# Delta rule's triangular inverse: diagonal blocks of 16 eliminated row by row on VectorE for all heads and segments at once

## The chip, the cores and the metric

The kernel runs on one core of a Trainium2 chip, in one launch. The metric is the device time of that core in microseconds (us); lower is better. Five engines work side by side: TensorE (PE) multiplies matrices, VectorE (DVE) and ScalarE (ACT) work elementwise and read out what TensorE left, GpSimd (POOL) does little here, and SyncE (SP) issues the DMAs. Engines run their own instructions in order and wait for one another by semaphores.

## The reference

Two blocks of two layers each run over 256 tokens of width 1024 in float32. In the first block 16 meta tokens stand ahead, so a layer has 272. Its mixer joins two branches: sparse attention, whose keys an index of eight small heads selects, and the gated delta rule with four heads of 128 and a per-token decay. The change is in the delta rule of the first block's two layers. Cut to what matters, per chunk and head:

```python
kk = einsum('bhncd,bhnsd->bhncs', kc, kc)
m = where(strict, bc[..., None] * kk * decay, 0.0)    # strictly lower
lhs = m + eye(CHUNK)
sol = triangular_solve(lhs, rhs, lower=True, unit_diagonal=True)
...                                  # then a scan over the chunks carries the state S
```

The result does not depend on the length of a chunk. The kernel uses its own: three segments of 16, 128 and 128 tokens.

## The kernel before

**Dense products.** Nearly all of the time goes to products of weights with activations, tokens as columns. A weight comes by DMA in pieces of 1 MB (`raw`, two buffers). ScalarE copies a 128x1024 stretch as `whi` (L261), VectorE subtracts that from `raw` to get `wlo` (L262), four buffers each, and TensorE takes three products per 128x128 tile: `whi` with the high part of the activations, `whi` with the low part, `wlo` with the high part (L287, L288, L289). So one split on VectorE feeds eight products on L289.

**Side chains.** Everything else of a mixer is written as generators. The function `dense` calls `tick()` twice per block of 128 output columns, and each tick takes every running chain to its next `yield`. So a chain's instructions stand in each engine's queue between dense products, in the order of the ticks. The projections are issued in the order of this line (L1077), where `k`, `q`, `v` are the delta rule's projections through a short convolution, `i` the index's queries, `b`, `K` and `kv` the attention's, `S` starts the attention's chain, `D` the delta rule's, and `g` and `z` are gates:

```python
for name in (begin + " k1 g1 q0 g2 q1 D i0 i1 S kv K v0 b0 v1 b1 g3 z0 z1 g4 g5 g6 g7").split():
```

After them the branch products follow, first the attention's, then (once all chains have ended) the delta rule's.

**The delta rule.** The chain `delta` waits for the sums of squares of q and k and makes their scales. Then it takes `part1(0)` and `scan(0)` for the 16 tokens, `part1(1)` and `part1(2)` in turn (a step of the one, a step of the other, then a yield for both), `scan(1)` and `scan(2)`. In `part1(s)` a step is four small float32 products, one for each head, into one PSUM bank `psn` (of which there are two), and an operation on VectorE or ScalarE that reads it:

1. the decays DT from the cumulated gates, four products, four VectorE operations, an exponential;
2. kk, and four VectorE operations that make MT, the transposed strictly lower matrix;
3. the inverse of (I + M), transposed as XT. It starts from the pairs (masks `lev1` and the identity), transposes to Xm (L752), and then takes a radix round (L765 with mask `rad`, then three steps of L771 with subtractions L775, L776) that joins four blocks into one: on blocks of 2 and on blocks of 8 for the large segments, on blocks of 2 alone for the 16-token one. Each round ends with a transposition. A half level joins blocks of 32 (of 8 in the small segment) by two product steps (L797 the first), and in the large segments a transposition and two more product steps join the two halves of 64;
4. q times k under the decays, then a wait until all of v is there, and transpositions of v and k.

Every yield of both large segments together costs one tick. The scan (from L849) then carries the state. The index (`index`, L632) adds eight scores per query tile on VectorE, from buffers of its own, `rl` (two) and `sc` (three).

The Tile framework places semaphores and keeps the order of the program on each engine, up to what its scheduler moves by data that is not yet there.

## Time and profile before

| what | before |
|---|---|
| median of three runs | 1631.58 us (1629.08 to 1631.98) |
| profiled execution, own time | 1631.2 us |
| its span in the trace | 1629.4 us |
| PE, busy | 1611.3 us, 99% |
| VectorE, busy | 1246.8 us, 77% |
| ScalarE, busy | 890.1 us, 55% |
| DMA, mean rate | 157 GB/s over the span |
| mean granted clock of PE | 0.991 |

Busy time is a sum over the span. PE and PEld (its weight loads) are pipelined, so a PE that is busy need not be at its peak. Where a row of the timeline shows a duration, the next instruction may start before its end; the distance from start to start is then the better price, and both are used below. The table by stretch gives, for each stretch of time, its length, the busy time of PE, PEld, VectorE, ScalarE and POOL with the instructions in brackets, then the clock that PE was granted (1.00 is full, one half is its lower level), the share of the DMA engines and their rate. A bracket at the end of a row of the timeline is the idle time just before, and what ended it. One float32 product is two records (x2) in a row's count, a transposition one.

### The profile page before, as it was taken

How to read it: one execution, taken by the hardware profiler on the slowest of the kernel's cores; microseconds unless marked ns; L12 is line 12 of the kernel's file. 1: busy time of each engine (PE TensorE's matmuls, PEld its weight loads, DVE VectorE, ACT ScalarE, POOL GpSimd, SP SyncE). 2: the span in 40 equal slices, each digit the busy share in tenths (PEclk: the TensorE clock that was granted, in tenths of full speed). 3: DMA queues.
4: the chain of work that ended last, by engine and by line, in shares of the span. 5: the costliest groups of instructions: out<-in, count | busy, mean ns of one | idle time of the engine just before them, and what ended most of it. 6: DMA issues, size and time to landing. Idle time of an engine off the chain costs nothing.

```text
span 1629.4 us, 30001 instructions
## 1 busy us (share of the span) xinstructions
PE 1611.3 (99%) x11806; PEld 1505.1 (92%) x11806; DVE 1246.8 (77%) x2715; ACT 890.1 (55%) x1556; POOL 18.0 (1%) x174
## 2 busy tenths in 40 slices
PE   7999999999999999999999999999999999999999
PEld 7989999999999989999998898899988888899997
DVE  6787568888557797588887649899956767789974
ACT  5665455555445664556665446566644444556652
POOL 0000000000000000000000000000000000000000
PEclk9998999999999999999999999999999999999999
DMA  5431224445553422245555553455555454545553
GB/s 207 155 110 73 104 99 161 169 171 179 169 181 130 155 104 79 79 147 170 193 191 179 200 180 126 160 182 188 185 183 194 158 178 155 174 169 192 190 183 128
DMA packets 38445, 257.89 MB, mean 158 GB/s; under 512 B 4384, under 2 KB 6816, under 8 KB 9120
## 3 DMA queue, kind: packets, MB, share of 16 engines
q1 hardware_dynamic: 37440, 253.79, 45.1%
q8 instruction: 93, 1.52, 0.4%
q10 hardware_dynamic: 864, 2.18, 0.3%
q14 instruction: 48, 0.39, 0.1%
HBM read 254.90 MB, written 1.05 MB: 157 GB/s over the span
## 4 chain that ended last, share of the span: by engine, by line
PE 96%; DVE 2%; ACT 1%; issue 0%; DMA 0%; SPq 0%; DVEq 0%; ACTq 0%
PE psd L289 20%; PE psd L287 19%; PE psd L288 18%; PE pss L285 5%; PE psn L285 5%; PE psd L285 3%; PE pss L289 3%; PE psn L289 3%; PE psn L771 1%; PE stat L500 1%; PE psd L352 1%; PE psd L353 1%; PE psd L354 1%; PE psn L353 1%; PE psn L352 1%; PE psn L354 1%
## 5 line engine op out<-in xcount | busy, mean ns | idle before, releaser
L261 ACT ACTIVATE whi<-raw 128x1024 fp32r<-128x1024 f32 (+1 forms) x487 | 508.3, 1044 | 546.6 <-PE psd L288 285.4
L262 DVE TENSOR_TENSOR wlo<-raw,whi 128x1024 fp32r<-128x1024 f32 (+1 forms) x487 | 585.2, 1202 | 206.9 <-ACT whi L261 202.6
L289 PE MATMUL psd<-x,wlo 128*128 128x256 f32 (+2 forms) x2384 | 682.5, 286 | 0.8 <-DVE wlo L262 0.8
L287 PE MATMUL psd<-x,whi 128*128 128x256 f32 (+2 forms) x2208 | 644.3, 292 | 7.0 <-ACT whi L261 6.3
L288 PE MATMUL psd<-x,whi 128*128 128x256 f32 (+2 forms) x2208 | 631.0, 286 | 0.0
L289 PEld LDWEIGHTS psd<-x,wlo 128*128 128x128 f32 x2384 | 451.9, 190 | 2.1 <-DVE wlo L262 1.3
L287 PEld LDWEIGHTS psd<-x,whi 128*128 128x128 f32 x2208 | 419.5, 190 | 15.7 <-ACT whi L261 6.3
L288 PEld LDWEIGHTS psd<-x,whi 128*128 128x128 f32 x2208 | 420.5, 190 | 3.0 <-issue 1.7
L289 PE MATMUL pss<-ax,wlo 128*128 128x256 f32 (+1 forms) x352 | 99.2, 282 | 0.0
L289 PE MATMUL psn<-ax,wlo 128*128 128x256 f32 (+1 forms) x352 | 99.2, 282 | 0.0
L285 PE MATMUL pss<-ax,whi 128*128 128x512 f32 x264 | 92.5, 394 | 0.0
L285 PE MATMUL psn<-ax,whi 128*128 128x512 f32 x264 | 92.5, 394 | 0.0
L289 PEld LDWEIGHTS psn<-ax,wlo 128*128 128x128 f32 x352 | 66.2, 188 | 0.0
L289 PEld LDWEIGHTS pss<-ax,wlo 128*128 128x128 f32 x352 | 66.2, 188 | 0.0
L285 PE MATMUL psd<-x,whi 128*128 128x512 f32 x176 | 61.7, 393 | 0.0
L285 PEld LDWEIGHTS pss<-ax,whi 128*128 128x128 f32 x264 | 49.6, 188 | 11.6
L285 PEld LDWEIGHTS psn<-ax,whi 128*128 128x128 f32 x264 | 49.6, 188 | 11.5
L389 ACT ACTIVATE gy<-gu,prm 128x256 f32<-128x256 f32 (+1 forms) x88 | 43.6, 500 | 4.0 <-DVE gu L386 3.8
L391 DVE SCALAR_TENSOR_TENSOR gy<-gu,prm,gy 128x256 f32<-128x256 f32 (+1 forms) x88 | 42.5, 485 | 1.7
L390 DVE SCALAR_TENSOR_TENSOR gy<-gu,prm,gy 128x256 f32<-128x256 f32 (+1 forms) x88 | 42.3, 483 | 0.9 <-ACT gy L389 0.9
L386 DVE TENSOR_TENSOR gu<-psd,rB 128x256 f32<-128x256 f32 (+2 forms) x88 | 37.0, 424 | 5.0 <-PE psd L289 3.7
L285 PEld LDWEIGHTS psd<-x,whi 128*128 128x128 f32 x176 | 33.0, 188 | 7.0
(404 smaller groups left out, 2497.2 us busy)
## 6 DMA issues: line engine op xcount, KB each, us to landing
raw<-in_w_up_dram SPq DMA_DIRECT2D x44, 1024.0 KB, 4.8
raw<-in_ffn_w_up_dram SPq DMA_DIRECT2D x44, 1024.0 KB, 4.7
raw<-in_w_in_dram SPq DMA_DIRECT2D x26, 1024.0 KB, 4.8
raw<-in_w_gate_dram SPq DMA_DIRECT2D x16, 1024.0 KB, 4.8
raw<-in_w_down_dram SPq DMA_DIRECT2D x16, 1024.0 KB, 4.9
raw<-in_ffn_w_down_dram SPq DMA_DIRECT2D x16, 1024.0 KB, 4.9
raw<-in_even_w_in_dram SPq DMA_DIRECT2D x10, 1024.0 KB, 4.8
raw<-in_w_out_dram SPq DMA_DIRECT2D x8, 1024.0 KB, 4.8
```

Of the source, the lines that this page charges most:

```text
L261: self.nc.scalar.activation(hi, src, AF.Copy)
L262: self.nc.vector.tensor_tensor(lo, src, hi.bitcast(F32), OP.subtract)
L285: mm(ps.rearrange("p (a n) -> p a n", a=2), w[0], x, start=first, stop=False)
L287: mm(ps, w[0], hi, start=first, stop=False)
L288: mm(ps, w[0], lo, start=False, stop=False)
L289: mm(ps[:, :n], w[1], hi, start=False, stop=last)
L352: mm(ps[m], h, hi[:, k, :], start=(kk == 0), stop=False)
L353: mm(ps[m], h, lo[:, k, :], start=False, stop=False)
L386: V.tensor_tensor(u[:, 2:2 + n], ps, N.rB, OP.mult)
L389: A.activation(y, u[:, o:o + T], AF.Copy, scale=conv(0, c))
L390: V.scalar_tensor_tensor(y, u[:, o + 1:o + 1 + T], conv(1, c), y, OP.mult, OP.add)
L391: V.scalar_tensor_tensor(y, u[:, o + 2:o + 2 + T], conv(2, c), y, OP.mult, OP.add)
```

## The change

The inverses of all three segments are made in one go, as far as blocks of 16. Right after its scales the chain runs `decays` for the three segments (steps 1 and 2 of above), which also gathers the eight diagonal blocks of each matrix: a mask product and a reduction leave, for each row, the 16 columns of its own block. Twelve pairs of head and segment then stand in one tile `diag` of 128x12x16. `eliminate` scales 15 shrinking parts of it on ScalarE, each by one column of a repeated 16x16 identity, in groups of 3, 4 and 8; for each group one float32 product with the block mask `blk` (504, 504 and 432 columns) spreads the scaled rows to all rows of their block. Fifteen pairs of VectorE operations follow (a product and a subtraction, of 12x15 columns down to 12x1), five groups of three with a yield after each. For the 16-token segment that is the whole inverse. For the large ones `part1` lays the blocks out in XT by one masked operation, and then takes one transposition, one radix round on 16 and the step on 64; the radix rounds on 2 and 8 and the half level on 32 are gone. The scores of the index lose their buffers and use two halves of two tiles `pT0`, `pT1` that the attention needs later. Line numbers of helpers are lower by 4 in the new kernel: the split is L258, the dense products are L283, L284, L285.

```diff
+B = 16
+NB = P // B
-RADIX, LEVELS = (2, 8), (8, 32)
...
+        two = [mp.tile([P, 2, SEQ], F32, tag=f"pT{j}", name=f"ix{j}") for j in range(2)]
...
-            rl = mp.tile([P, SEQ], F32, tag="rl", name="rl", bufs=2)
+            rl = two[0][:, hh % 2, :]
...
-            na = mp.tile([P, SEQ], F32, tag="sc", name="sc", bufs=3)
+            na = two[1][:, hh % 2, :]
...
-    def part1(s):
+    diag = quad("vs", 2).rearrange("p h n -> p (h n)")[:, :12 * B].rearrange("p (h r) -> p h r", h=12)
+    slot = {0: 8, 1: 0, 2: 4}
+
+    def decays(s):
...
+        own = diag[:, slot[s]:slot[s] + 4, :]
+        if s:
+            W = quad("W", 2)
+            V.tensor_tensor(W, MT, mid(c["blk"], 4), OP.mult)
+            V.tensor_reduce(own, W.rearrange("p h (b r) -> p h r b", r=B), AX.X, OP.add)
+        else:
+            G.memset(own, 0.0)
+            A.activation(own[:n], MT[:n], AF.Copy)
+        yield
+    XD = dn.tile([P, 12, B], F32, tag="XD", name="XD")
+    def eliminate():
+        views = []
+        for tag, group in (("od", range(0, 3)), ("vt", range(3, 7)), ("ks", range(7, B - 1))):
+            low, o = quad(tag).rearrange("p h n -> p (h n)"), 0
+            for j in group:
+                m = B - 1 - j
+                views.append(low[:, o:o + 12 * m].rearrange("p (h r) -> p h r", h=12))
+                A.activation(views[j], diag[:, :, j + 1:], AF.Copy, scale=c["idb"][:, j:j + 1])
+                o += 12 * m
+            ps = k_.ps("n")
+            mm(ps[:, :o], c["blk"], low[:, :o], start=True, stop=True)
+            A.activation(low[:, :o], ps[:, :o], AF.Copy)
+            yield
+        V.tensor_copy(XD, mid(c["idb"], 12))
+        Y = quad("Y", 2).rearrange("p h n -> p (h n)")
+        for j in range(B - 1):
+            m = B - 1 - j
+            t = Y[:, :12 * m].rearrange("p (h r) -> p h r", h=12)
+            V.tensor_tensor(t, views[j], XD[:, :, j:j + 1].to_broadcast([P, 12, m]), OP.mult)
+            V.tensor_tensor(XD[:, :, j + 1:], XD[:, :, j + 1:], t, OP.subtract)
+            if j % 3 == 2:
+                yield
+    def part1(s):
...
+        own = XD[:, slot[s]:slot[s] + 4, :]
+        if s:
...
+            V.tensor_tensor(XT.rearrange("p h (b r) -> p h b r", r=B),
+                            own.unsqueeze(2).to_broadcast([P, 4, NB, B]),
+                            c["blk"].rearrange("p (b r) -> p b r", r=B).unsqueeze(1).to_broadcast([P, 4, NB, B]),
+                            OP.mult)
...
-        for w in RADIX:
-            if 4 * w > n:
-                break
...
-        Y = quad("Y", 2)
-        G.memset(Y[:n, :, :n], 0.0)
-        py = k_.ps("n")
-        for hh in range(4):
-            mm(half(py)[:, hh, :], MT[:n, hh, :n], par(Xm, 0)[:, hh], start=True, stop=True)
...
-        pt = k_.ps("n")
-        for hh in range(4):
-            mm(half(pt)[:, hh, :], Y[:n, hh, :n], par(XT, 1)[:, hh], start=True, stop=True)
-        V.tensor_tensor(par(XT, 1), par(XT, 1), half4(pt), OP.subtract)
...
+        else:
+            XT = own
...
+        yield from in_turn(decays(0), decays(1), decays(2))
+        yield from eliminate()
         yield from part1(0)
         yield from scan(0)
         yield from in_turn(part1(1), part1(2))
```

Where the instructions stand now is shown at three places. On VectorE in layer 0, before, the small segment's radix steps (`Y`, `W`, `XT`, 16 rows) stand with the splits (`wlo`) and the rotation of the index's queries (`iq`, `iqb`):

```order
L765 TENSOR_TENSOR Y<-psn,g_93 16x4x16
L623 TENSOR_TENSOR iq_1094<-psd,g_93 128x256
L624 TENSOR_TENSOR iqb<-iqb,g_93 128x256
L775 TENSOR_TENSOR W<-XT,psn 16x4x2x4
L625 TENSOR_TENSOR iq_1094<-iq_1094,iqb 128x256
L776 TENSOR_TENSOR XT<-XT,psn 16x4x2x2
L262 TENSOR_TENSOR wlo<-raw,whi 128x1024
L775 TENSOR_TENSOR W<-XT,psn 16x4x2x2
```

After, in the same part of the layer (`Y`, `XD`: the elimination; `ix`: the index's scores; `kT`: the attention's keys; `uka`, `rka_y`: small scales of the keys):

```order
L778 TENSOR_TENSOR Y<-od,XD 128x180
L674 SCALAR_TENSOR_TENSOR uka<-stat,epu 128x3
L779 TENSOR_TENSOR XD<-XD,Y 128x12x15
L248 TENSOR_SCALAR rka_y<-uka 128x3
L258 TENSOR_TENSOR wlo<-raw,whi 128x1024
L642 SCALAR_TENSOR_TENSOR ix_1201<-ix_1200,aabw,g_93 128x128
L778 TENSOR_TENSOR Y<-od,XD 128x168
L642 SCALAR_TENSOR_TENSOR ix_1201<-ix_1200,aabw,ix_1201 128x128
L779 TENSOR_TENSOR XD<-XD,Y 128x12x14
L667 TENSOR_TENSOR kT<-ropex,g_93 128x272
L778 TENSOR_TENSOR Y<-od,XD 128x156
```

What was an operation on 16 rows between two splits is now one on 128 rows and 12x15 columns downwards, and the index's scores run beside it.

On PE in layer 0, before, the small segment's last radix step (L771) and the index's products (`ikT`, L639) stand between dense products:

```order
L288 MATMUL psd<-x_119,whi 128x272
L289 MATMUL psd<-x_119,wlo 128x272
L771 MATMUL psn<-W,Y 16x2x2 x4
L639 MATMUL pss<-ikT,iq_978 128x128 x2
L287 MATMUL psd<-x_98,whi 128x272
L288 MATMUL psd<-x_98,whi 128x272
L289 MATMUL psd<-x_98,wlo 128x272
```

After, there are two spreading products (L770, from the scaled parts `od` and `vt`) one behind the other, with sums of squares (`stat`, L496) and dense products ahead:

```order
L496 MATMUL stat<-g_77,sqm 16x1
L496 MATMUL stat<-g_77,sqm 128x1 x2
L283 MATMUL psd<-x_98,whi 128x272
L284 MATMUL psd<-x_98,whi 128x272
L770 MATMUL psn<-od,g_93 128x504
L770 MATMUL psn<-vt,g_93 128x504
L285 MATMUL psd<-x_98,wlo 128x272
L283 MATMUL psd<-x_101,whi 128x272
```

The second spreading product stands directly behind the first; nothing of other work lies between them.

On PE in layer 0, before, a step of the radix round (L771, blocks of 8: 24 columns of each of 4 groups) stands among the dense products:

```order
L287 MATMUL psd<-x_107,whi 128x272
L288 MATMUL psd<-x_107,whi 128x272
L289 MATMUL psd<-x_107,wlo 128x272
L771 MATMUL psn<-XT,Y 128x4x24 x8
L953 MATMUL pss<-kT,bq_1494 128x272
L287 MATMUL psd<-x_110,whi 128x272
L288 MATMUL psd<-x_110,whi 128x272
L289 MATMUL psd<-x_110,wlo 128x272
```

After, the round is on blocks of 16 (L819), and a transposition of the scan's output (L932) stands ahead of it:

```order
L932 MATMUL psn<-g_77,od 128x16 x4
L819 MATMUL psn<-XT,Y 128x2x48 x8
L283 MATMUL psd<-x_110,whi 128x272
L284 MATMUL psd<-x_110,whi 128x272
L285 MATMUL psd<-x_110,wlo 128x272
L819 MATMUL psn<-W,Y 128x2x32 x4
L283 MATMUL psd<-x_113,whi 128x272
```

Two steps of the round now have three dense products between them, where before six and a score product of the attention (`pss`, L953) stood about one step.

## Rows read from the trace of the kernel before

**Rows 1.** The page: PE's busy time, its 40 slices, the last chain.

```profile
PE 1611.3 (99%) x11806; PEld 1505.1 (92%) x11806; DVE 1246.8 (77%) x2715; ACT 890.1 (55%) x1556; POOL 18.0 (1%) x174
...
PE   7999999999999999999999999999999999999999
...
PE 96%; DVE 2%; ACT 1%; issue 0%; DMA 0%; SPq 0%; DVEq 0%; ACTq 0%
```

**Rows 2.** By stretch: length, busy us of PE, PEld, DVE, ACT, POOL; PEclk.

```profile
77.00:99.00 22.00, 22.00 (x219) 19.55 (x218) 16.78 (x60) 14.48 (x35) 0.20 (x2) 1.00 0.33 110
99.00:131.00 32.00, 31.79 (x244) 28.35 (x244) 31.25 (x106) 21.72 (x48) 0.20 (x2) 1.00 0.26 97
131.00:151.00 20.00, 20.00 (x124) 17.99 (x122) 12.51 (x42) 8.61 (x20) 0.00 (x0) 0.74 0.16 53
151.00:190.00 39.00, 39.00 (x314) 37.27 (x313) 29.24 (x96) 17.37 (x36) 1.05 (x2) 1.00 0.30 109
603.00:620.00 17.00, 17.00 (x128) 15.87 (x127) 13.69 (x49) 8.07 (x19) 0.00 (x0) 0.90 0.18 63
```

**Rows 3.** PE's timeline, layer 0: start, us, what, count; large segments' steps.

```profile
174.23 1.92 PE L771 MATMUL psn<-XT,Y 128*128 128x96 f32 x16
175.98 0.65 PE L953 MATMUL pss<-kT,bq 128*128 128x272 f32 x2
...
185.51 1.03 PE L752 MATMUL psn<-g,XT 128*128 128x128 f32 x8
...
188.34 1.89 PE L797 MATMUL psn<-X,MT 128*128 128x64 f32 x16
```

**Rows 4.** PE's timeline, layer 0: two steps of the 16-row segment.

```profile
84.27 0.25 PE L752 MATMUL psn<-g,XT 16*16 16x16 f32 x4
...
86.24 0.36 PE L771 MATMUL psn<-XT,Y 16*16 16x12 f32 x8
```

**Rows 5.** PE's timeline in the last mixer: two f32 products of 512 columns.

```profile
1271.02 1.02 PE L1374 MATMUL pss<-v,a 128*128 128x512 f32 x2
1271.88 1.02 PE L1376 MATMUL pss<-v,a 128*128 128x512 f32 x2
```

**Rows 6.** VectorE's groups by line: busy us, mean ns, idle before.

```profile
L735 DVE SCALAR_TENSOR_TENSOR MT<-psn,bet,QT 128x128 f32<-128x128 f32 x16 | 5.0, 334 | 3.6 <-PE psn L732 3.6
...
L775 DVE TENSOR_TENSOR W<-XT,psn 128x256 f32<-128x256 f32 x8 | 3.4, 422 | 4.0 <-PE psn L771 4.0
...
L1187 DVE TENSOR_REDUCE emx<-att 128x1 f32<-128x256 f32 x8 | 3.2, 410 | 0.1
...
L739 DVE TENSOR_TENSOR XT<-MT,g 128x512 f32<-128x512 f32 x4 | 2.7, 678 | 0.0
```

**Rows 7.** VectorE's timeline: small operations, and the two tightest splits.

```profile
80.69 0.17 DVE L928 TENSOR_TENSOR bet<-g_r,ruk 128x12 f32<-128x12 f32 x1
80.77 0.17 DVE L255 TENSOR_TENSOR nwt_b<-nwt_a,uqk 128x12 f32<-128x12 f32 x1
...
126.46 1.21 DVE L262 TENSOR_TENSOR wlo<-raw,whi 128x1024 fp32r<-128x1024 f32 x1
...
594.29 1.21 DVE L262 TENSOR_TENSOR wlo<-raw,whi 128x1024 fp32r<-128x1024 f32 x1
```

**Rows 8.** PE's timeline: first use of these two splits, and one wait.

```profile
128.90 0.29 PE L289 MATMUL psd<-x,wlo 128*128 128x272 f32 x1
...
129.77 0.39 PE L875 MATMUL psn<-vs,XT 16*16 16x128 f32 x2 [0.21 <-ACT vs L832]
...
601.38 0.29 PE L289 MATMUL psd<-x,wlo 128*128 128x260 f32 x1
```

**Rows 9.** VectorE's waits, 77 to 131 us: the longest kind.

```profile
DVE uqk L920 <- PE stat L500: 1.3, 1, 1.3
```

**Rows 10.** ScalarE's groups by line: a scaled copy.

```profile
L841 ACT ACTIVATE ks<-psn,g_E 128x128 f32<-128x128 f32 x8 | 2.2, 347 | 0.0
```

**Rows 11.** PE's timeline at the branch products of layer 1.

```profile
709.81 0.63 PE L287 MATMUL psd<-o,whi 128*128 128x260 f32 x3 [1.34 <-ACT o L261]
```

77 lines of the change are left out of this document (29 added, 48 removed).

## The prediction

> **What bounds the kernel now.** I read the page first: TensorE (PE) shows work for 1611.3 of the 1629.4 us span, VectorE (DVE) for 1246.8, ScalarE (ACT) for 890.1, and 96% of the chain that ended last runs over PE [rows 1]. PE's digits are 9 in every slice but the first [rows 1], so there is hardly an idle stretch to win: a product that is taken away is time, and one that is added is time. Next, the table by stretch [rows 2]: in the mixers too PE is busy all the time, but VectorE's share swings. From 99 to 131 us (layer 0; top-k masks, conv, rope beside the dense products) VectorE works 31.25 of 32 us; from 151 to 190 us, where the delta rule's large blocks run, 29.24 of 39. And twice the granted clock falls: 0.74 over 131 to 151 us and 0.90 over 603 to 620 us, both where the first segment's 16-row products stand. So the question has three parts: what PE saves, whether VectorE can carry its share where it is put, and what the clock does.
>
> **TensorE, removed.** In segments 1 and 2 the radix round on blocks of 2 goes (the one on 16 has the form of the old one on 8), so does the half level on 32, and two of the four transposes to Xm. Four heads and two segments make 16 records for one step of products and 8 for a transpose step. Such a step of 96 columns is shown with 1.92 us from 174.23 on, but the next product starts at 175.98: the end overlaps by 0.17, and the step costs 1.75. One of 64 columns (1.89 shown) costs 1.72 by the same overlap, a transpose step (1.03 shown) 0.86 [rows 3]. The columns hardly matter, so I take 1.73 for all. Per layer: radix round 4 steps, 6.9; level 32 two steps, 3.5; two transposes, 1.7: 12.1 us. For the 16-row segment six product steps and two transposes go; they show 0.36 and 0.25 us [rows 4]; with some 0.07 of overlapped end off each that is 2.1 us. Together 14.2 us per layer, 28.4 us in two layers.
>
> **TensorE, added.** Three spreading products per layer, of 504, 504 and 432 columns in f32. A 512-column f32 product took 1271.02 to 1271.88, 0.86 us [rows 5]; 0.86 + 0.86 + 0.73 = 2.45 us a layer, 4.9 in all. The decay and kk products of segments 1 and 2 are only moved ahead. Net on PE: 28.4 - 4.9 = 23.5 us less.
>
> **VectorE, total.** Removed per layer: per large segment two masks of 512 columns (0.678 us each, [rows 6]), one radix round (one product mask, and five subtractions of up to 256 columns, 0.42 at most) and the level's two of 256; with the first segment's ten small ones some 10 to 11 us. Added: two masks, two reductions, two spreads of 512 columns, and 30 small operations. For these I go by start to start: a 12-column operation starts 0.08 us after the one before, though it is shown with 0.17 [rows 7], and a 512-column one is 0.678 - 0.08 = 0.60 us, so 1.04 ns a column. The 30 operations have 2 x 12 x (15 + ... + 1) = 2880 columns: 30 x 0.072 + 3.0 = 5.2 us. If each had to wait for its predecessor's end, since it reads what that wrote, it would be at most 30 x 0.157 + 3.0 = 7.7 (0.157 is the 0.17 less its 12 columns). In total VectorE is about even. What matters is where it stands.
> The Trainium skill, page "VectorE: DVE Perf Modes", section "The TRN2 errata", speaks against this change: every instruction on SBUF pays a fixed latency, so many small tiles pay it many times, and it advises tiles of 512 elements and more. Its (N + 151) / 0.96 ns would make the 30 operations 7.7 us, an estimate from that page; the sum below would end some 2 to 4 us later by it. [rows 7] bear out the duration and not the spacing, since the ends overlap.
>
> **VectorE, moved.** All of this now comes before the values are there, in the stretch that was full. Ahead of the split that ends the squeeze it adds, per layer: the 16 decay and kk operations of segments 1 and 2 (0.334 shown, 0.26 start to start: 4.2 us, [rows 6]), masks and reductions (4 x 0.60 = 2.4; a strided reduction of 512 has no row, the 256-column one at 0.41 us scales to 0.6 to 0.7), the elimination 5.2, less 1.1 for the first segment: 10.7 us (13.2 with the long price). PE has more to do there as well: the moved products (two steps of 1.73 at most) and 2.45, less 2.1: 3.8 us. What stands behind VectorE's queue is the split of the next weights (wlo); PE needs each, and four buffers limit the lead. Counted off in order (each split feeds eight products), the tightest of layer 0 ran from 126.46 to 127.67 and was first used at 128.90: 1.2 us of slack [rows 7, 8]. In layer 1 it ended at 595.50 and was used at 601.38: 5.9 us [rows 7, 8]. VectorE's idle time of 77 to 131 us, 54 - 48.0 = 6.0 us [rows 2], lies in waits, the longest 1.3 us for the sums of q and k [rows 9]; it may be filled, wholly or not at all. Layer 0: 1.2 + 3.8 - 10.7 = -5.7 without and +0.3 with the idle time, so PE waits 0 to 5.7 us; layer 1: -1.0 to +5.0, so 0 to 1.0. I take the middles, 2.9 and 0.5: 3.4 us given back. With the long price and nothing filled it is 8.2 + 3.5 = 11.7.
>
> **A new hand-off.** Each spreading product is written right behind the ScalarE scalings that it reads (3, 4, 8 of them), without a tick between, and PE is in order: behind it wait the dense products. A scaled ScalarE copy of 128 columns took 0.347 us [rows 10]; overlapped about 0.25, so the groups take 0.9, 1.1 and 1.7 us, 3.7 a layer if PE always came first. The order puts PE's dense rows ahead of two of the three, and only the second stands directly behind the first. I take 1 us a layer, bounds 0 and 3.7: 2 us. ScalarE itself has room: 36 of 54 us busy from 77 to 131 [rows 2], and some 5 us are added.
>
> **Edits that I cost at nothing.** The score buffers of the index (two halves of two tiles): the relu copies keep two buffers, and the scores are written and read on VectorE alone. The smaller constants: one load. The second half of the delta rule gets fewer steps in a row (10 ticks in place of 20), and its end comes earlier. This has one small gain: in layer 1 PE waited 1.34 us at 709.81 for the first branch product, whose input hung on the delta rule's last output [rows 11]. With the delta rule done ahead of the last gates that goes: -1.3 us. The large steps now follow each other with fewer dense rows between; PE's order has a product ready wherever one is missing, as before.
>
> **The clock.** Low stretches cost 20 x 0.26 = 5.2 us in layer 0 and 17 x 0.10 = 1.7 in layer 1 [rows 2]. The first segment's 16-row scan products ahead of them stay. I take no change; bounds: all 6.9 regained, or as much again lost.
>
> **Sum**, against the profiled execution's 1631.2 us (span 1629.4 and 1.8 around it; the runs' median is 1631.58, so I shift nothing): 1631.2 - 28.4 + 4.9 + 3.4 + 2.0 - 1.3 = 1611.8. I say 1612.
>
> **Rivals.**
> 1. *The cover holds and the clock comes back.* VectorE fills its idle time, ScalarE is ahead, and the work that stood in the slow stretch is gone or spread: 1631.2 - 23.5 - 1.3 - 6.9 = 1599.5. For it: the clock fell where thin products stood together, and the products that ran at half clock there move to 80 us. Against it: the scan's products stay.
> 2. *VectorE becomes the bound of its stretch.* Dependent pairs at full length, no idle time filled, every hand-off paid: 11.7 + 7.4 in place of 3.4 + 2.0, so 1625.5. For it: 31.25 of 32 us. Against it: in layer 1 the slack was 5.9 us.
> 3. *Slower: the clock falls wherever PE now waits.* Place: the elimination's stretch and the crowded small steps of both layers. A us at half clock loses half a us, as 131 to 151 us show; the gain of 20 us is gone from 40 us of further low clock, 20 in each layer; with 26 in each, 1638. For it: the clock fell at 131 us though PE had waited only 0.21 us there [rows 8], so thin work suffices. Against it: 151 to 190 us, with the same kinds of small step, ran at 1.00 [rows 2]. The Trainium skill ("TensorE: Matmul & The Clock Gate", "Why this matters for your kernels") has the clock halve after idle gaps; by that rule the waits above would be paid nearly twice, 1617, which no row here shows.
> That the change doesn't do what it says is no rival: PE's order has the steps removed.
>
> **How the numbers follow.** Forecast 1604 to 1619: 0.58. Rival 1 (1596 to 1604): 0.15. Rival 2 (1619 to 1628): 0.16. Rival 2 with some loss of clock, about 1630: 0.05. Rival 3: 0.06. The range takes in the forecast and most of rivals 1 and 2: 1600 to 1625. A difference of 0.2%, 3.3 us, is about what a measurement of this kernel can tell from none. Faster: 0.58 + 0.15 + 0.15 = 0.88, trimmed to 0.85 for what I have not seen; the same 0.08; slower 0.07.
>
> **What would show it.** Right: PE's records for the radix step halve, its small steps cost some 12 us less a layer, VectorE is full from 77 to 131 us, and PE waits a few us for wlo there, more in layer 0 than in layer 1. Wrong: waits for wlo of over 10 us, long waits of the 504-column products for ScalarE, or further stretches of granted clock under 1.

## The result and the profile after

The changed kernel took 1612.51 us in the median of four executions (1609.75 to 1618.88), against 1630.33 us for the kernel before beside it (1628.91 to 1631.98). The ratio is 0.9896, 95% interval 0.9861 to 0.9931; a second set of runs gave 0.9893 (0.9876 to 0.9909). The forecast was 1612 in a range of 1600 to 1625. The profiled execution of after took 1609.75 us, with a span of 1607.9 at a mean granted clock of 0.993; that of before had 1631.2, 1629.4 and 0.991. So the medians differ by 17.8 us, where the sum of the forecast had 19.4, and the pair of traces by 21.5: the execution of after that was traced is the fastest of its four.

The page of after, as in [rows 1] (busy time of each engine; PE's digits; the chain that ended last):

```profile
PE 1587.6 (99%) x11482; PEld 1477.2 (92%) x11482; DVE 1247.1 (78%) x2729; ACT 897.4 (56%) x1582; POOL 16.1 (1%) x170
...
PE   7999999999999999999999999999999999999998
...
PE 93%; DVE 4%; ACT 2%; issue 0%; DMA 0%; DVEq 0%; SPq 0%; ACTq 0%
```

TensorE's busy time fell by 23.7 us (1611.3 to 1587.6), VectorE's stayed (1246.8 and 1247.1). The table by stretch, columns as in [rows 2]:

```profile
77.00:99.00 22.00, 21.96 (x169) 18.92 (x168) 19.60 (x70) 17.34 (x46) 0.20 (x2) 1.00 0.20 57
99.00:131.00 32.00, 31.21 (x203) 26.54 (x202) 28.32 (x104) 16.10 (x37) 0.20 (x2) 0.89 0.27 94
131.00:151.00 20.00, 19.58 (x156) 17.68 (x155) 18.30 (x58) 14.73 (x36) 0.00 (x0) 1.00 0.30 103
560.00:603.00 43.00, 41.19 (x275) 35.16 (x274) 38.18 (x124) 24.02 (x52) 0.20 (x2) 0.92 0.22 74
603.00:620.00 17.00, 17.00 (x132) 16.47 (x130) 13.26 (x54) 8.99 (x26) 0.00 (x0) 0.90 0.51 172
```

The stretch from 131 to 151 us, at 0.74 before, is at 1.00 now, and 99 to 131 us has fallen to 0.89. In layer 1 a second low stretch has joined (560 to 603 us, 0.92); the one of 603 to 620 us stays at 0.90. VectorE works 19.60 of 22 us from 77 to 99 us (16.78 before), 28.32 of 32 from 99 to 131 (31.25 before) and 18.30 of 20 from 131 to 151 (12.51 before): its load came forward and also went on after 131 us. From 77 to 131 us it is busy for 47.92 of the 54 us, as before (48.03).

Now PE's timeline where waits stand, in layer 0 and in layer 1 (start, us, what, count; in brackets the wait and what ended it):

```profile
107.76 1.00 PE L362 MATMUL pss<-g,rka_y 16*128 16x16 f32 x6 [0.40 <-DVE rka_y L252]
108.59 0.49 PE L685 MATMUL pss<-g,vraw 128*16 128x128 f32 x3
109.29 3.57 PE L637 MATMUL pss<-ikT,iq 64*128 64x256 f32 x8 [0.20 <-DVE kT L680]
112.78 0.59 PE L285 MATMUL psd<-x,wlo 128*128 128x272 f32 x1
...
564.69 1.00 PE L362 MATMUL pss<-g,rka_y 16*128 16x16 f32 x6 [1.11 <-DVE Y L778]
565.52 0.49 PE L685 MATMUL pss<-g,vraw 128*16 128x128 f32 x3
566.22 3.14 PE L637 MATMUL pss<-ikT,iq 64*128 64x256 f32 x8 [0.20 <-DVE kT L680]
```

No row waits for wlo. Instead, PE's order sets other things ahead of the next wlo product: the products that spread the keys' scales (L362), transpositions of v (L685) and the index's scores (L637, eight records in one go, 3.57 and 3.14 us). In the kernel before the index's products of 256 columns came four by four, as in this row, most of them at 0.70 us:

```profile
107.83 0.70 PE L639 MATMUL pss<-ikT,iq 64*128 64x256 f32 x4
```

The waits in brackets, 0.40 and 0.20, 1.11 and 0.20 us, are waits for VectorE's queue. Below, "the index's products are held" says that these records take longer from start to start than they did before.

To compare kernels I use one account of PE. Each matmul record is given the time from its start to the next one's start. Taken off are idle time and, where the clock was low, half of the time there; what is left goes to the dense products (those with whi or wlo) or to all others. Layer 0 runs from the 121st to the 377th product with wlo of the trace, layer 1 from the 1121st to the 1425th, which are the same products in every kernel. "Low clock" is the time so taken off. Us:

| kernel, layer | length | idle | low clock | dense | others |
|---|---|---|---|---|---|
| before, 0 | 175.5 | 0.6 | 5.1 | 106.5 | 63.2 |
| after, 0 | 163.5 | 1.4 | 3.4 | 104.5 | 54.2 |
| before, 1 | 187.3 | 1.4 | 1.7 | 121.3 | 62.9 |
| after, 1 | 179.5 | 2.1 | 5.1 | 118.9 | 53.4 |

Layer 0 became 12.0 us shorter, layer 1 7.8; together 19.8 of the traces' 21.5. Of these, the small products gave 18.5, the dense ones 4.4; idle time took back 1.4 and the clock 1.7.

### The profile page after: what moved, and what is told of

Same layout as the page of the kernel before. It is cut to its first block, busy times and chain, and to the rows that moved or that the text cites. A ratio compares the mean times of both kernels' runs of the same rounds, so it can differ in the third digit from the quotient of the medians.

```text
span 1607.9 us, 29362 instructions
## 1 busy us (share of the span) xinstructions
PE 1587.6 (99%) x11482; PEld 1477.2 (92%) x11482; DVE 1247.1 (78%) x2729; ACT 897.4 (56%) x1582; POOL 16.1 (1%) x170
## 3 DMA queue, kind: packets, MB, share of 16 engines
HBM read 254.78 MB, written 1.05 MB: 159 GB/s over the span
## 4 chain that ended last, share of the span: by engine, by line
PE 93%; DVE 4%; ACT 2%; issue 0%; DMA 0%; DVEq 0%; SPq 0%; ACTq 0%
PE psd L285 19%; PE psd L283 18%; PE psd L284 18%; PE pss L281 5%; PE psn L281 5%; PE psd L281 3%; PE pss L285 3%; PE psn L285 3%; PE stat L496 1%; PE psd L348 1%; PE psd L349 1%; PE psd L350 1%; DVE wlo L258 1%; PE psn L349 1%; PE psn L348 1%; PE psn L350 1%
## 5 line engine op out<-in xcount | busy, mean ns | idle before, releaser
L258 DVE TENSOR_TENSOR wlo<-raw,whi 128x1024 fp32r<-128x1024 f32 (+1 forms) x487 | 585.7, 1203 | 207.6 <-ACT whi L257 202.4
L285 PE MATMUL psd<-x,wlo 128*128 128x256 f32 (+2 forms) x2384 | 683.4, 287 | 0.8 <-DVE wlo L258 0.8
L283 PE MATMUL psd<-x,whi 128*128 128x256 f32 (+2 forms) x2208 | 642.7, 292 | 7.6 <-ACT whi L257 6.9
L284 PE MATMUL psd<-x,whi 128*128 128x256 f32 (+2 forms) x2208 | 631.4, 286 | 0.0
L285 PEld LDWEIGHTS psd<-x,wlo 128*128 128x128 f32 x2384 | 452.3, 190 | 4.2 <-DVE wlo L258 1.6
L283 PEld LDWEIGHTS psd<-x,whi 128*128 128x128 f32 x2208 | 419.9, 190 | 15.5 <-ACT whi L257 6.9
L284 PEld LDWEIGHTS psd<-x,whi 128*128 128x128 f32 x2208 | 421.1, 191 | 3.3 <-issue 1.7
L285 PE MATMUL psn<-ax,wlo 128*128 128x256 f32 (+1 forms) x352 | 99.2, 282 | 0.0
L285 PE MATMUL pss<-ax,wlo 128*128 128x256 f32 (+1 forms) x352 | 99.2, 282 | 0.0
L285 PEld LDWEIGHTS psn<-ax,wlo 128*128 128x128 f32 x352 | 66.2, 188 | 0.0
L285 PEld LDWEIGHTS pss<-ax,wlo 128*128 128x128 f32 x352 | 66.2, 188 | 0.0
L281 PEld LDWEIGHTS pss<-ax,whi 128*128 128x128 f32 x264 | 49.5, 188 | 11.3
L281 PEld LDWEIGHTS psn<-ax,whi 128*128 128x128 f32 x264 | 49.5, 188 | 11.3
L410 DVE TENSOR_TENSOR a<-vy,s 128x256 f32<-128x256 f32 (+1 forms) x88 | 37.5, 427 | 2.5 <-ACT s L396 0.5
```

Of the source, the lines that this page charges most:

```text
L258: self.nc.vector.tensor_tensor(lo, src, hi.bitcast(F32), OP.subtract)
L281: mm(ps.rearrange("p (a n) -> p a n", a=2), w[0], x, start=first, stop=False)
L283: mm(ps, w[0], hi, start=first, stop=False)
L284: mm(ps, w[0], lo, start=False, stop=False)
L285: mm(ps[:, :n], w[1], hi, start=False, stop=last)
L410: V.tensor_tensor(a, y, G[m], OP.mult)
```

## The experiments

Ratios are to the kernel before in the same set of runs; the changed kernel is at 0.9893 to 0.9896. A difference of 0.001 is 1.6 us. The 95% intervals reach 0.0013 to 0.0035 to either side, so 2 to 3 us between two kernels are at the edge of what the ratios can tell.

**The changed kernel again.** Unchanged.

> The changed kernel itself, to see how far its executions differ and with what clock. Theory A (the granted clock makes the difference): span times mean granted clock is the same in each execution within 2 us, about 1595 us, as in the four shown so far (1607.9 x 0.993 = 1596.6, 1617.1 x 0.986 = 1594.5), and the median lies between 1609 and 1617. Theory B (waits or transfers make it): the product differs by as much as the times, up to 9 us.

1612.06 us (1610.51 to 1615.24), ratio 0.9893 (0.9876 to 0.9909). Span times granted clock, for all eight executions of the changed kernel:

| time | 1609.75 | 1610.10 | 1610.51 | 1611.36 | 1612.76 | 1614.93 | 1615.24 | 1618.88 |
|---|---|---|---|---|---|---|---|---|
| clock | 0.993 | 0.991 | 0.992 | 0.991 | 0.990 | 0.989 | 0.988 | 0.986 |
| span x clock | 1596.6 | 1593.8 | 1595.8 | 1595.1 | 1594.9 | 1595.5 | 1594.1 | 1594.5 |

The times differ by 9.1 us, the products by 2.8, of which the rounding of the clock to 0.001 can make 1.6. Theory A holds but for its margin: what differs between executions of this kernel is how long the clock was low. For the seven executions of before beside them the product lies between 1614.1 and 1615.7. Within one kernel it can serve as its work at full clock: 1595.0 and 1614.5, so the change took away 19.5 us of work, and the mean clock fell from some 0.992 to 0.990. Between kernels with other stalls it can't be used so plainly, since a low clock need cost nothing where PE waits anyway.

**The elimination's VectorE operations left out** (XD then stays the identity):

```diff
-            t = Y[:, :12 * m].rearrange("p (h r) -> p h r", h=12)
-            V.tensor_tensor(t, views[j], XD[:, :, j:j + 1].to_broadcast([P, 12, m]), OP.mult)
-            V.tensor_tensor(XD[:, :, j + 1:], XD[:, :, j + 1:], t, OP.subtract)
```

> The 30 VectorE operations of the elimination (L778, L779) are left out of each layer; all else, the yields too, stays. Theory A (PE's own work sets the time, VectorE's load is covered but for the waits that the trace shows: 0.4 + 0.4 + 0.2 us in layer 0, 1.1 + 0.4 + 0.3 + 0.2 in layer 1): 1 to 3 us less, and up to 7 more where the low clock behind those waits (109.9 to 116.8, 567.3 to 574.2) goes with them. Theory B (VectorE's queue holds PE up by late splits): 2 x 5.2 = 10 us or more, at the same clock. Theory C (the thin products there bring the low clock, not the waits): the low stretches stay, and the gain is 1 to 2 us.

1608.32 us, ratio 0.9866 (0.9850 to 0.9883): 3.7 us less than the changed kernel by the medians, 4.4 by the ratios, for 10.4 us of VectorE. Idle time and other products fell from 1.4 + 54.2 to 0.5 + 52.9 in layer 0 and from 2.1 + 53.4 to 0.7 + 51.2 in layer 1, together 5.7 us: the waits went, and the index's products were no longer held. The dense products took 1.7 more. The two low stretches that stood behind the waits went, at 110 and at 567 us; another came in layer 0, where the kernel before had its own, from 137.6 to 147.8 us, with one wait of 0.2 us before it:

```profile
99.00:131.00 32.00, 31.85 (x239) 27.97 (x240) 30.74 (x90) 21.18 (x46) 0.20 (x2) 1.00 0.38 134
131.00:151.00 20.00, 19.75 (x120) 17.20 (x120) 13.30 (x37) 11.63 (x33) 0.00 (x0) 0.74 0.31 106
```

So VectorE's load there costs about 4 us (3.0 by span times clock, 1592.0 against 1595.0), not nothing and not 10: theory A for the cost. For the clock neither theory holds: the low stretches went with the waits, and one came without.

**One pair a tick.**

```diff
-            if j % 3 == 2:
-                yield
+            yield
```

> The elimination yields after each pair of operations in place of each third, so its 30 operations spread over 15 ticks; no operation is added or left out. Theory A (the waits for the keys' scales come from the burst of elimination ahead of them): the waits of PE for rka and kT get under 0.3 us, the low stretches behind them go, 3 to 7 us less. Theory C (thin products bring the low clock): same time within 2 us. Theory D (the delta rule now ends too late): PE waits at the first branch product of layer 1 again, 1 to 5 us more.

1615.53 us, ratio 0.9909 (0.9894 to 0.9924), 3.5 us slower by the medians and 2.6 by the ratios. All theories but D missed the sign, and D names the wrong place: there is no wait at the branch product. PE waits of the kernel, layer 0 (what waits, for what: total, times, longest):

```profile
PE psd L285 <- DVE wlo L258: 3.5, 3, 2.3
```

Here is the wait that the prediction had named for the change itself: PE stands at wlo, 3.5 us in layer 0 and 2.8 in layer 1. The elimination then lasts into the convolution of v (in layer 0 its last operation starts at 133.7 us, in the changed kernel at 111.7), and the splits come late. The waits for the keys' scales are gone as expected, and the other products, the index's above all, take 1.0 and 2.3 us less, against 5.2 us more of idle time. Span times clock is 1595.5, as in the changed kernel (1595.0), so by that measure the difference is clock (0.988 to 0.991). So the crowd on VectorE is real, and the order decides where it shows.

**Before, with fewer steps** (the large segments' inverse is then incomplete): in the loop over the radix, blocks of 2 are skipped for 128 rows, the transposition after blocks of 8 is left out, and the half level runs for 16 rows alone.

```diff
+            if n == P and w == 2:
+                continue
...
+            if n == P:
+                break
             untranspose(n)
...
-        Y = quad("Y", 2)
+        if n < P:
+            Y = quad("Y", 2)
```

> The kernel before, with the radix round on 2, the half level on 32 and two transpositions left out for the large segments (their output is then not the inverse), and nothing put in their place. Prediction's price: 2 x 12.1 = 24.2 us less, 1606. If the dense products also run closer together without them, as the changed kernel's trace shows (2.0 and 2.4 us less a layer for the dense products), 28 us less. If other work fills in and the steps were partly hidden: under 18 us less.

1603.35 us, ratio 0.9836 (0.9821 to 0.9851): 25.8 us less by the medians, 26.7 by the ratio. In the account the other products give 11.3 and 11.4 us a layer (63.2 to 51.9, 62.9 to 51.5), where 12.1 was predicted; the dense ones give 1.6 and 1.4 (106.5 to 104.9, 121.3 to 119.9), which the prediction had not priced. Together 25.7; span times clock gives 1588.5 against 1614.5 (means of four and seven executions), 26.0. In the trace of this kernel the low clock of layer 0 is gone too:

```profile
99.00:131.00 32.00, 31.79 (x244) 28.40 (x244) 31.34 (x106) 21.60 (x49) 0.20 (x2) 1.00 0.26 98
131.00:151.00 20.00, 20.00 (x164) 18.65 (x164) 16.54 (x59) 10.24 (x24) 0.00 (x0) 1.00 0.15 53
```

There is no fall at 131 us, though the first segment's 16-row products stand there as before. Its four executions had 0.991 to 0.993, hardly more than those of before (0.990 to 0.992).

**The whole elimination in one tick.**

```diff
-            if j % 3 == 2:
-                yield
```

> The other way: the elimination's 15 pairs are written in one tick, without a yield between. Same instructions. Theory E (the later the elimination ends, the more it falls on the splits and the convolution of v; one pair a tick was 3.5 us slower than three): 1 to 4 us less than the changed kernel's 1612, with no waits for wlo. Theory F (a burst ahead of the splits holds them up): waits for wlo of 2 us or more, 2 to 5 us more.

1613.09 us, ratio 0.9890 (0.9878 to 0.9903): no difference. Both theories missed. PE's waits for the keys' scales grew (1.1 and 1.7 us), waits for wlo didn't come.

**The elimination on GpSimd.**

```diff
-            V.tensor_tensor(t, views[j], XD[:, :, j:j + 1].to_broadcast([P, 12, m]), OP.mult)
-            V.tensor_tensor(XD[:, :, j + 1:], XD[:, :, j + 1:], t, OP.subtract)
+            G.tensor_tensor(t, views[j], XD[:, :, j:j + 1].to_broadcast([P, 12, m]), OP.mult)
+            G.tensor_tensor(XD[:, :, j + 1:], XD[:, :, j + 1:], t, OP.subtract)
```

> The 30 operations of the elimination run on GpSimd in place of VectorE; all else as in the changed kernel. Theory A (their cost is VectorE's time in the crowded stretch): 3 to 4 us less than 1612, as with the operations left out (1608.3). Rival G (the chain gets longer than its cover: the 30 dependent operations take several us more there): PE waits at the first product with the inverse of the first segment, 2 to 20 us more. Rival H (GpSimd slows VectorE beside it): VectorE's operations get longer in 95 to 115 us, no gain.

1611.56 us (1608.91 to 1623.31, clock 0.986 to 0.996), ratio 0.9892 (0.9868 to 0.9915): nothing gained. Two rows of its VectorE timeline, one of GpSimd's groups (busy us, mean ns, idle before), and two of its waits in layer 1:

```profile
94.92 1.46 DVE L258 TENSOR_TENSOR wlo<-raw,whi 128x1024 fp32r<-128x1024 f32 x1
...
100.15 0.73 DVE L668 TENSOR_TENSOR ropeb<-ropeb,g 128x272 f32<-128x272 f32 x1
...
L778 POOL TENSOR_TENSOR Y<-od,XD 128x168 f32<-128x168 f32 x1 | 0.5, 503 | 0.1
...
DVE XT L790 <- POOL xp L591: 8.8, 1, 8.8
...
PE psd L285 <- DVE wlo L258: 4.6, 1, 4.6
```

The same operations took VectorE 0.43 us (272 columns) and 1.22 (the split) in the changed kernel; here up to 0.73 and 1.46 (from 92 to 113 us 0.52 and 1.33 in the mean). So rival H is right in part. A page of the Trainium skill bears on this: "SBUF — State Buffer", section "Terms", has VectorE and GpSimd share a pair of ports that one of them holds for a whole instruction. The longer VectorE rows agree with that; no run here shows that the ports are their cause. GpSimd needs 0.50 us for 168 columns, VectorE 0.33, and the 60 operations show 30.6 us on GpSimd. Rival G is right too, at another place than it named: in layer 1 VectorE stood for 8.8 us at the operation that lays out XT (L790), until GpSimd's elimination had ended (the row names the small fill that stands right behind it on GpSimd). The next split stood behind it in VectorE's order, and PE waited 4.6 us for that. In both layers together PE's idle time rose by 6.4 us against the changed kernel's trace, and the low clock cost 6.2 less.

**The large segments' part later.** The first segment gets an elimination of its own, that of the large ones stands behind its scan.

```diff
-        yield from in_turn(decays(0), decays(1), decays(2))
-        yield from eliminate()
+        yield from decays(0)
+        yield from eliminate(16, 4, [("od", range(0, B - 1))], 3, "XD0")
         yield from part1(0)
         yield from scan(0)
+        yield from in_turn(decays(1), decays(2))
+        yield from eliminate(P, 8, [("od", range(0, 4)), ("vt", range(4, 12)), ("ks", range(12, B - 1))], 5, "XD")
         yield from in_turn(part1(1), part1(2))
```

> The first segment gets an elimination of its own (4 heads, 16 rows, one spreading product of 480 columns); decays, masks, reductions, spreading products (432, 480, 48 columns) and elimination of the two large segments stand behind the first segment's scan, five pairs a tick, where VectorE had room before. PE has the same work within 0.5 us a layer, VectorE 2 us more in all. Theory A (what the changed kernel gives back is VectorE's crowd before v): 3 to 6 us less than 1612. Rival I (the delta rule now ends after its cover): PE waits before the delta rule's branch product in layer 1 again and the small steps crowd, 0 to 4 us more. Rival J (the place doesn't matter, since other products fill in): within 1.5 us.

1612.37 us, ratio 0.9887 (0.9872 to 0.9901): rival J's number, but not for its reason. The clock stayed at 1.00 in all four stretches of the mixers:

```profile
99.00:131.00 32.00, 31.32 (x220) 26.91 (x219) 29.74 (x91) 19.28 (x41) 0.20 (x2) 1.00 0.31 107
131.00:151.00 20.00, 18.88 (x145) 16.66 (x144) 18.11 (x68) 12.46 (x31) 0.00 (x0) 1.00 0.16 55
560.00:603.00 43.00, 42.18 (x321) 37.34 (x320) 40.69 (x135) 28.19 (x64) 0.20 (x2) 1.00 0.29 99
603.00:620.00 17.00, 15.65 (x101) 12.60 (x101) 16.35 (x56) 12.88 (x39) 0.00 (x0) 1.00 0.37 123
```

so the 8.5 us that low clock had cost in the account went; in exchange idle time rose to 2.8 and 4.1 us (one wait of 1.3 us before the delta rule's branch product among it, as in [rows 11]), and the dense products took 108.4 and 121.1 us, 3.9 and 2.2 more than in the changed kernel. For that see the visits, below.

**No spreading products** (the scaled rows are not spread):

```diff
-            ps = k_.ps("n")
-            mm(ps[:, :o], c["blk"], low[:, :o], start=True, stop=True)
-            A.activation(low[:, :o], ps[:, :o], AF.Copy)
+            A.activation(low[:, :o], low[:, :o], AF.Copy)
```

> The three spreading products of each layer are left out (ScalarE copies the scaled rows onto themselves in their place). Prediction: 4.9 us for the products and 2.0 for the hand-off from ScalarE, 6.9 less. By the trace of after, where PE waited 0.3 us for these scalings in one layer and not in the other: 4.9 + 0.3 = 5.2 less.

1609.33 us (1606.00 to 1613.69), ratio 0.9869 (0.9852 to 0.9886): some 3 to 4 us less, not 5.2 or 6.9. By span times clock nothing of that is work (1594.9 against 1595.0); the clock was 0.990 to 0.995. The other products fell by 2.4 and 3.4 us, but idle time rose by 2.8 and 2.7, and the dense products by 0.1 and 1.3. PE's waits in layer 1:

```profile
PE pss L362 <- DVE XD L777: 3.6, 1, 3.6
PE psd L285 <- DVE wlo L258: 1.3, 2, 0.7
```

PE waited 3.6 us for VectorE at the keys' scales (3.4 in layer 0). In layer 0 it came to them at 109.1 us, VectorE had them at 112.4; in the changed kernel these were 107.4 and 107.6. Work taken from PE in this stretch came back as waits: VectorE bounds it. VectorE's operations also stand in another order here, so how much of the wait is the order's is not shown.

**The keys' chain later.**

```diff
         ra = k_.rsqrt(ua, 3, "rka")
-        yield
+        for _ in range(4):
+            yield
```

> The changed kernel with three more yields in the attention's key chain between its scales (rka) and the products that spread them (L362); nothing else. PE waited 0.4 and 1.1 us there. Theory K (only PE's order is at fault: a product stands too early): 2 to 5 us less than 1612, no wait for rka, and no new one. Theory L (VectorE bounds this stretch, and PE is out of dense work whatever stands there): the idle time turns up at wlo or at the index's products, within 1.5 us of 1612.

1607.14 us (1606.64 to 1607.77), ratio 0.9852 (0.9837 to 0.9866): 5 us less than the changed kernel by the medians, 6.7 by the ratios. It beats both kernels. The wait for rka is gone, another at wlo has come (1.5 us in layer 0, 1.2 in layer 1), so both theories saw a part of it:

```profile
PE psd L285 <- DVE wlo L258: 1.5, 1, 1.5
```

Idle time is 1.8 and 2.0 us, much as in the changed kernel; other products fell by 1.3 and 2.9 us, since the index's products no longer stand in one go (they come in twos and fours, at 0.70 us). Span times clock is 1592.4, 2.6 less than the changed kernel's; the rest of the 5 us is clock. All four executions had 0.992, where the changed kernel's eight had 0.986 to 0.993. In the trace the low clock cost nothing in layer 0 and 8.5 us in layer 1.

**No gathering of the diagonals** (the elimination works on other data):

```diff
-            V.tensor_tensor(W, MT, mid(c["blk"], 4), OP.mult)
-            V.tensor_reduce(own, W.rearrange("p h (b r) -> p h r b", r=B), AX.X, OP.add)
+            A.activation(own, MT[:, :, :B], AF.Copy)
```

> The masks and reductions that gather the diagonal blocks (L748, L749, 0.60 and 0.95 us from start to start, twice a layer: 6.2 us of VectorE in all) are left out; ScalarE copies 64 columns of MT in their place. Theory L (VectorE bounds the stretch before v, and its work there costs about 4 of 10, as the elimination did): 2 to 3 us less than 1612. Theory A (covered, but for the waits): within 1 us.

1603.91 us, ratio 0.9835 (0.9819 to 0.9851), 8 to 9.5 us less: more than any theory, and more than the 6.2 us of VectorE that went. Its trace has no low clock in either mixer:

```profile
99.00:131.00 32.00, 31.72 (x235) 27.58 (x234) 29.99 (x109) 18.46 (x43) 0.20 (x2) 1.00 0.20 67
131.00:151.00 20.00, 19.55 (x153) 17.66 (x153) 18.38 (x62) 13.08 (x31) 0.00 (x0) 1.00 0.35 112
560.00:603.00 43.00, 42.42 (x320) 36.79 (x319) 39.94 (x127) 26.50 (x64) 0.20 (x2) 1.00 0.29 99
603.00:620.00 17.00, 16.61 (x148) 15.24 (x146) 12.60 (x46) 9.04 (x20) 0.00 (x0) 1.00 0.43 133
```

Idle, dense and other products together are 160.5 and 175.2 us against 160.1 and 174.4 in the changed kernel: no gain at all. The whole difference is the clock, 8.5 us in the traces; span times clock is 1594.9 against 1595.0. Why it held here stays open; the numbers that are multiplied are other ones too.

**The keys' chain later, and the masked product in another layout.**

```diff
-            V.tensor_tensor(W, MT, mid(c["blk"], 4), OP.mult)
-            V.tensor_reduce(own, W.rearrange("p h (b r) -> p h r b", r=B), AX.X, OP.add)
+            V.tensor_tensor(W.rearrange("p h (r b) -> p h b r", r=B), MT.rearrange("p h (b r) -> p h b r", r=B),
+                            c["blk"].rearrange("p (b r) -> p b r", r=B).unsqueeze(1).to_broadcast([P, 4, NB, B]), OP.mult)
+            V.tensor_reduce(own, W.rearrange("p h (r b) -> p h r b", r=B), AX.X, OP.add)
```

> As e9, and the masked product writes its 512 columns so that the reduction reads each sum's eight values side by side: the reduction should take 0.6 in place of 1.0 us, if its stride made it long, and 1.6 us of VectorE go in both layers together. Theory L: 0.5 to 1 us less than e9. If the product's strided write takes as much longer, no difference.

1608.13 us, ratio 0.9856 (0.9841 to 0.9871): no difference from the one before. VectorE's groups of the two operations (busy us, mean ns), first the changed kernel's, then this one's:

```profile
L749 DVE TENSOR_REDUCE vs<-W 128x64 f32<-128x512 f32 x2 | 2.1, 1035 | 0.0
...
L748 DVE TENSOR_TENSOR W<-MT,g 128x512 f32<-128x512 f32 x2 | 1.4, 684 | 0.0
```

```profile
L749 DVE TENSOR_TENSOR W<-MT,g 128x512 f32<-128x512 f32 x2 | 2.4, 1196 | 0.0
...
L751 DVE TENSOR_REDUCE vs<-W 128x64 f32<-128x512 f32 x2 | 1.3, 673 | 0.0
```

The reduction took 673 in place of 1035 ns, the product 1196 in place of 684. The stride costs the one that walks it (the product also reads its operands in runs of 16 here).

**The keys' chain later, and the index's own buffers.**

```diff
-            rl = two[0][:, hh % 2, :]
+            rl = mp.tile([P, SEQ], F32, tag="rl", name="rl", bufs=2)
...
-            na = two[1][:, hh % 2, :]
+            na = mp.tile([P, SEQ], F32, tag="sc", name="sc", bufs=2)
```

> As e9 (the keys' chain later), with the index's scores back in buffers of their own (two and two, not three, for which the memory doesn't suffice beside the new constants). Prediction's term (the shared halves cost nothing): the same ratio as e9, 0.985, within 0.001. Rival (the halves of pT0 and pT1 tie the index to the attention, and the longer waits for the relu copies seen after the change, 2.1 in place of 1.1 us, come from them): 1.5 us less or more.

1608.59 us, ratio 0.9852 (0.9832 to 0.9872), the ratio of the kernel with the later keys. The shared halves cost nothing that the time shows, as the prediction had them. The interval is too wide for the 1.5 us of the rival, but nothing speaks for it: span times clock is 1596.1 with buffers of their own, 3.7 more than with the shared halves, and the waits for wlo in layer 0 rose from 1.5 to 3.1 us.

## Why the prediction was right, and where its steps were not

**TensorE, removed: right.** 12.1 us a layer for the large segments; 11.3 and 11.4 were measured by leaving out just these steps. What lay on PE came off the time almost one to one. The first segment's 2.1 us were not measured alone.

**Missing from the sum: the visits.** A visit is a group of small products between two dense ones, and it costs more than its own products:

```profile
98.43 0.29 PE L284 MATMUL psd<-x,whi 128*128 128x272 f32 x1
98.55 0.29 PE L285 MATMUL psd<-x,wlo 128*128 128x272 f32 x1
98.77 0.49 PE L637 MATMUL pss<-ikT,iq 64*128 64x128 f32 x4
99.19 0.39 PE L285 MATMUL psd<-x,wlo 128*128 128x272 f32 x1
99.42 0.29 PE L283 MATMUL psd<-x,whi 128*128 128x272 f32 x1
```

Here the dense product at 98.43 took 0.12 us from start to start, the one ahead of the small products 0.22 and the one behind them 0.23. In the mean, over both layers of before and after, a dense product between dense ones takes 0.12 to 0.13 us, one with a small product behind it 0.16 to 0.17, the first one after small products 0.23 to 0.25. So each visit of small products costs about 0.16 us of dense time (0.05 and 0.11). Before there were 62 visits in layer 0 and 65 in layer 1, after 52 and 48. 10 and 17 visits less are 1.6 and 2.7 us; 2.0 and 2.4 were measured. In the kernel with the large part later there are 65 and 61, 13 more each, and the dense products take 3.9 and 2.2 us more than in the changed kernel, where 13 visits would be 2.1. A straight line through all fourteen traces has 0.24 us of dense time for a visit in layer 0 (0.18 without that kernel) and 0.15 in layer 1.

**TensorE, added: right in price.** The three products show 1.01, 1.11 and 0.99 us, against 1.02 for one of 512 columns in [rows 5]:

```profile
92.44 1.01 PE L770 MATMUL psn<-od,g 128*128 128x504 f32 x2
93.49 1.11 PE L770 MATMUL psn<-vt,g 128*128 128x504 f32 x2
...
96.47 0.99 PE L770 MATMUL psn<-ks,g 128*128 128x432 f32 x2
...
548.13 1.11 PE L770 MATMUL psn<-od,g 128*128 128x504 f32 x2 [0.31 <-ACT od L767]
```

But in its stretch PE does not bound alone: leaving them out took nothing off span times clock (1594.9 against 1595.0). Without them PE waits for as long. That a product is time wherever it stands was the rule of the prediction, and in this run it did not hold. In the account the small products of both layers fell by 18.5 us where the prediction's price was 28.4 - 4.9 = 23.5. Of the 5.0 us between, 1.5 are the steps' price (24.2 against 22.7) and 3.0 the index's products that were held (below).

**VectorE, total: right for the elimination.** All 60 operations of both layers, each from its start to the next one's, less idle time, are 10.4 us, where 2 x 5.2 were forecast. One of 144 columns took 0.21 us and one of 12 columns 0.09:

```profile
88.15 1.05 DVE L749 TENSOR_REDUCE vs<-W 128x64 f32<-128x512 f32 x1
89.12 0.68 DVE L748 TENSOR_TENSOR W<-MT,g 128x512 f32<-128x512 f32 x1
...
95.64 1.22 DVE L258 TENSOR_TENSOR wlo<-raw,whi 128x1024 fp32r<-128x1024 f32 x1
...
99.51 0.30 DVE L778 TENSOR_TENSOR Y<-vt,XD 128x144 f32<-128x144 f32 x1
99.72 0.43 DVE L669 TENSOR_TENSOR kT<-kT,ropeb 128x272 f32<-128x272 f32 x1
...
110.11 1.22 DVE L258 TENSOR_TENSOR wlo<-raw,whi 128x1024 fp32r<-128x1024 f32 x1
111.25 0.17 DVE L778 TENSOR_TENSOR Y<-ks,XD 128x12 f32<-128x12 f32 x1
111.34 0.44 DVE L601 SCALAR_TENSOR_TENSOR v<-th,yv 128x272 f32<-128x272 f32 x1
```

(0.072 + 144 x 0.00104 = 0.22, 0.072 + 0.012 = 0.08.) Other work stands between any two dependent ones, so the long price never came up. It does exist: in the kernel with the large part later, 11 of 120 stand right ahead of the one that reads their result, and that one starts 0.03 us after their end. The Trainium skill's formula ("VectorE: DVE Perf Modes", "The TRN2 errata") fits the durations shown (0.17 for 12 columns), not the spacing, as the prediction had it. What was mis-sized is the reduction: it was taken for 0.6 to 0.7 us, from one along contiguous columns, and took 1.05, 0.97 from start to start.

**VectorE, moved: the amount was near, the way was not.** 3.4 us of waits for wlo were predicted; there were none. VectorE was not full from 77 to 131 us either (47.9 of 54 us, as before): the idle time that the prediction took as half filled stayed. After the split at 95.64 the next one is at 110.11 us, 14.5 us later, but PE's order has other ready products ahead of its use. The squeeze itself did come. Counted off as in the prediction, eight products a split, the tightest split up to 131 us had 0.5 us of slack in layer 0 (1.2 before), and the tightest of layer 1 had 0.05 (5.5 before):

```profile
595.20 1.22 DVE L258 TENSOR_TENSOR wlo<-raw,whi 128x1024 fp32r<-128x1024 f32 x1
...
596.15 0.70 PE L285 MATMUL psd<-x,wlo 128*128 128x272 f32 x2
```

The split ends at 596.41, and the second of the two PE records, the first that needs it, starts at 596.47. What came in place of the waits for wlo: 0.6 and 1.3 us of waits for the keys' scales and keys, and index products that stood in one go and took 1.3 and 1.7 us more (16 records of L637 with 256 columns, 2.8 to 4.0 us in layer 0 and 2.9 to 4.7 in layer 1, start to start at full clock). Together 4.9 us, near the 4 us that leaving the elimination out gave back. What holds the index's products is not shown by itself; where a wait before them is long enough to be listed, as with the elimination on GpSimd (2.9 us in layer 0), it is one for ScalarE's relu copies (L639). The step that failed is the claim of what stands behind VectorE's queue: the prediction looked only at the split, and the keys' chain and the index stood there as well. One pair a tick made the predicted wait come true.

**The hand-off: too dear.** 2.0 us were predicted (bounds 0 to 7.4); the only wait of a spreading product for ScalarE is 0.31 us, in layer 1.

**The tail: right.** The wait of 1.34 us before the delta rule's branch product is gone; it came back at 1.3 us in the kernel that ends the delta rule later.

**The clock: the unknown that is left.** No change was predicted, with bounds of 6.9 either way. In the traces of the mixers it took back 1.7 us, and about as much in the medians (19.5 us of work, 17 to 18 us of time); but between executions of the changed kernel it makes 9 us of difference. Rival 3's mechanism did happen, at a third of the point from which it decides: the clock fell in the elimination's stretch of both layers and cost 3.4 us each, where 10 each would have taken the gain. Rival 1's happened beside it: the fall at 131 us went (5.1 us). In all fourteen traces five waits of PE in the mixers are longer than 2 us, and near each a low stretch begins, in the wait or within 2 us of its end (us):

| kernel, layer | wait | until | low clock |
|---|---|---|---|
| one pair a tick, 0 | 2.33 | 137.6 | 139.1 to 142.5 |
| one pair a tick, 1 | 2.35 | 596.8 | 596.4 to 599.9 |
| elimination on GpSimd, 1 | 4.56 | 567.1 | 564.9 to 571.7 |
| no spreading, 0 | 3.45 | 112.6 | 112.5 to 115.9 |
| no spreading, 1 | 3.56 | 568.2 | 569.9 to 573.3 |

The Trainium skill's rule ("TensorE: Matmul & The Clock Gate", "Why this matters for your kernels") that idle gaps halve the clock agrees with these. But the two longest low stretches of layer 0, 10.2 us each, began with no wait above 0.25 us in the 4 us ahead (at 133.1 in the kernel before, at 137.6 without elimination), and the kernel with the large part later, whose waits add up to 2.8 and 4.1 us with none above 1.4, had no low clock in the account. After waits of 1 to 2 us there is sometimes a low stretch and sometimes none. What decides is not settled. The low stretch at 110 us lies at the index's products in one go in both executions of the changed kernel that have a trace, and in that with one tick; with the keys later it was gone in layer 0, but layer 1 had more of it, and with the other layout beside it a shorter one came back in layer 0.

**By layer** the errors met: layer 0 gave 12.0 us where the sum had 7.9 (14.2 less 2.45, 2.9 and 1.0), layer 1 7.8 where it had 11.6 (14.2 less 2.45, 0.5 and 1.0, and 1.3 more). So the total is right to 1 us in part by luck: the waits came out smaller and elsewhere, the visits were not counted, and the clock went the other way in each layer.

## What to carry to other kernels

Where one engine is busy all the time, price a removed step by what stands from start to start on that engine, and count the visits as well: a short step among dense products costs them something each time it comes. Where work is moved ahead on a second engine, look for everything that waits behind its queue, not only the most frequent reader; here a side chain of three small scales cost more than the splits, and letting it come three ticks later took 5 us off the median, about half of it work and the rest clock. Between executions compare the granted clock first.

## What the runs showed of the hardware that was not expected

The same program's mean clock lay between 0.986 and 0.993 from one execution to the next, which is 9 us of 1612. Near each of five waits of PE of over 2 us the clock fell, and it also fell where PE had waited no more than 0.25 us. A visit of small float32 products among dense ones costs about 0.16 us. A strided walk over 512 float32 elements made a VectorE operation longer by 0.36 us when it was read by a reduction (673 to 1035 ns) and by 0.51 when it was written by a product (684 to 1196). With GpSimd at work beside it, VectorE took up to 0.73 in place of 0.43 us for 272 columns, and it stood for 8.8 us behind one operation that waited for GpSimd.
